# A two-layer hybrid transformer on one core: log sigmoid with tokens on partitions, queries split in place, keys' tiles exchanged, and the first sum of squares taken tile by tile

## The chip, the core and the metric

The kernel runs on one core of one Trainium2 chip. The metric is device time in microseconds; lower is better. The engines of a core work through queues of their own, in order: TensorE (matrix products, with a separate queue entry for loading weights), VectorE, ScalarE, GpSimd, and SyncE, which here only issues DMAs. In the profile they are PE (and PEld for weight loads), DVE, ACT, POOL and SP. Everything is float32 in and out.

## The reference, cut to what matters

There are 512 tokens of width 1024 and two layers. Every layer is a norm, a mixing part, a norm, and a gated feed-forward part with a short convolution.

```python
def rmsnorm(x, g):
    y = xf * lax.rsqrt(jnp.mean(xf * xf, axis=-1, keepdims=True) + EPS) * g

# layer 0: 8 heads of "fox" attention and 8 heads of sparse attention (dsa)
log_f = jax.nn.log_sigmoid(ff + b_fox_f)          # 512 tokens x 8 heads
c = jnp.cumsum(log_f, axis=1)                     # over tokens
s = einsum(q, k) * scale + c_q - c_k              # fox: decay between query and key
score = einsum(iw, relu(einsum(iq, ik)))          # dsa: an index over keys, per query
_, sel = lax.top_k(score, 128)                    # only the best 128 keys take part
# layer 1: 16 heads of block attention (moba); with 512 tokens it is causal softmax attention
mq, mk = apply_partial_rope(mq), apply_partial_rope(mk)
```

A partial rotation (rope) by position is applied to the queries and keys of the dsa and moba heads and of the index, but not to the fox heads.

## The kernel before, in words

Features lie on partitions and tokens along the free axis: x is `xT`, eight tiles of 128 features by 512 tokens. Since float32 products go through TensorE as two reduced-precision halves, every operand is split into a high part (a cast on ScalarE) and a low part (the remainder, a subtraction on VectorE or GpSimd), and a product is three matmuls: high by high, high by low, low by high (`mm3`, lines 159 to 161). `proj` makes 128 output features for all tokens with 24 such matmuls of 512 columns. Its result lies in one of three PSUM tiles with the tag `mm`.

The norm is not applied to x ahead of the products. `prep` (lines 171 to 177) scales x by the gain and splits it into `xh` and `xl`; the factor per token, one over the root of the mean square, is multiplied in when a product leaves PSUM (`scaled`, or in `rope` through the tables `CR` and `SR`, which are the cosine and sine tables times that factor). The factor is made by `rstd_of`: four transposes of the sum of squares, a sum over the free axis, a handful of small VectorE instructions for the root (lines 195 to 201), and four transposes that spread it over the partitions.

At the start (lines 563 to 590) the eight tiles of x arrive by DMA. `rope_angles` reduces position times frequency to an angle with some 26 small VectorE instructions on 128x32 and 128x64 and takes the sine; `rope_tables` writes these into tables and transposes them. `square` sums squares of tiles 0 to 3 on GpSimd, the loop behind it those of 4 to 7 on VectorE, and `rstd_main` makes the factor. The first projection (`misc`) holds the index key, the shared rope key, the forget gate in rows 96 to 103 and the index weights in rows 104 to 107. `ym` is this tile after rope.

The log sigmoid of the forget gate is computed on rows 96 to 127 of `ym`, 512 tokens along the free axis (lines 645 to 655): absolute value, exponential, logarithm with a correction, then a running sum over tokens. The result and its remainder are copied into four groups of 32 rows of the tile `ck`, which enters the fox scores as a matmul of its own (line 344).

Heads are worked in pairs, two heads of 64 rows in one projection. `stack_q` makes two tiles from a pair's queries, each with one head's high parts in one half of the partitions and its low parts in the other: a cast and a subtraction over 128 rows, and three DMAs that move halves across partitions. `stack_k` makes four tiles from the keys with six DMAs: head 0 uses the tile in which the parts were made, once its upper half is overwritten, and head 1 a tile filled by two DMAs. `scores` (lines 268 and 269) then needs two matmuls per block. The DMAs are issued on SP's queue, as are the loads of weights.

`heads` writes a software pipeline: scores and softmax of one head, then projections of the next pair, then the mix of the head before. The index scores and the selection of 128 keys (`select`, VectorE's max and replace instructions, lines 629 and 630) are put between the fox heads. The instructions are written in this order, but their order in each engine's queue is set by a planner: it goes through the program with a cost model and gives each engine, of the instructions it believes ready, the one written first. At run time the queues are strictly in order.

## Time and profile before

| | us |
|---|---|
| median of 3 runs | 1263.99 (1262.1 to 1265.39) |
| the profiled execution | 1261.51, of it 1259.7 from its first to its last instruction |
| TensorE busy | 1220.4 (97%) |
| VectorE busy | 810.9 (64%) |
| ScalarE busy | 557.4 (44%) |
| GpSimd busy | 357.7 (28%) |

The attention part of the first layer lasts until about 265 us of the span, its feed-forward part until about 640, the attention part of the second layer until about 870, and its feed-forward part to the end. Busy time is a union of instructions; idle time in front of an instruction stands in brackets behind it with what ended it.

### The profile page before, as it was taken

The numbers are of one execution on the slowest core, as the hardware profiler recorded it, in microseconds if no ns is written. First come the engines' busy times: TensorE is split into PE (matmuls) and PEld (weight loads), VectorE is DVE, ScalarE is ACT, GpSimd is POOL, SyncE is SP. The second block draws the span as 40 slices with busy tenths as digits, with TensorE's granted clock in tenths as the row PEclk, the third lists the DMA queues.
The fourth block names the chain that finished last, engine by engine and source line by source line (L and its number), as shares of the span: only waits on it lengthen the run. The fifth ranks groups of instructions, "written<-read, shape, count | busy, mean of one in ns | idle before, by whom it ended". The sixth has DMA issues, their size and how long they took to land.

```text
span 1259.7 us, 16807 instructions
## 1 busy us (share of the span) xinstructions
PE 1220.4 (97%) x5996; PEld 1018.3 (81%) x5996; DVE 810.9 (64%) x1489; ACT 557.4 (44%) x969; POOL 357.7 (28%) x394
## 2 busy tenths in 40 slices
PE   6889999999999999999999999999999999999997
PEld 4768778778888888888887888888888888888887
DVE  7889988675654555544666778787655555444555
ACT  5564667653332333333445556555433333332334
POOL 3665557542111111111213223332222111111110
PEclk9989999999999999999999999999999999999999
DMA  5333444222333322323325434331233332333321
GB/s 194 101 92 111 128 99 128 63 80 89 101 100 100 98 90 93 96 93 100 103 96 142 113 100 123 105 109 67 84 93 108 100 100 92 94 100 101 96 88 67
DMA packets 57379, 127.24 MB, mean 101 GB/s; under 512 B 7584, under 2 KB 21024, under 8 KB 57296
## 3 DMA queue, kind: packets, MB, share of 16 engines
q1 hardware_dynamic: 56368, 124.81, 33.2%
q10 hardware_dynamic: 864, 1.17, 0.3%
q8 instruction: 47, 0.77, 0.2%
q14 instruction: 36, 0.29, 0.1%
q0 software_dynamic: 64, 0.20, 0.0%
HBM read 104.13 MB, written 2.10 MB: 84 GB/s over the span
## 4 chain that ended last, share of the span: by engine, by line
PE 79%; DVE 10%; issue 5%; ACT 3%; DMA 2%; POOL 1%; POOLq 0%; ACTq 0%; DVEq 0%; SPq 0%
PE mm_g L160 6%; PE mm_g L161 6%; PE mm_g L159 6%; PE mm_u L161 6%; PE mm_u L159 6%; PE mm_u L160 6%; PE mm_d L161 6%; PE mm_d L160 6%; PE mm_d L159 6%; DVE tmask L630 2%; DVE m L629 1%; DMA mq_l<-mq_h 1%; PE t_m L372 1%; PE o_m L381 1%; PE mm_mk L160 1%
## 5 line engine op out<-in xcount | busy, mean ns | idle before, releaser
L434 POOL TENSOR_TENSOR cv<-cv,gs 128x512 f32<-128x512 f32 x44 | 57.1, 1298 | 546.2 <-ACT gs L433 546.2
L159 PE MATMUL mm_d<-a_h,wh_d 128*128 128x512 f32 (+1 forms) x384 | 142.8, 372 | 0.0
L160 PE MATMUL mm_d<-a_l,wh_d 128*128 128x512 f32 (+1 forms) x384 | 142.6, 371 | 0.0
L161 PE MATMUL mm_d<-a_h,wl_d 128*128 128x512 f32 (+1 forms) x384 | 142.6, 371 | 0.0
L503 DVE TENSOR_TENSOR us<-mm_u,cv 128x512 f32<-128x512 f32 x44 | 30.4, 692 | 168.1 <-PE mm_u L161 132.7
L160 PE MATMUL mm_g<-xl,wh_g 128*128 128x512 f32 x352 | 137.2, 390 | 0.4 <-DVE xl L175 0.4
L159 PE MATMUL mm_u<-xh,wh_u 128*128 128x512 f32 x352 | 137.3, 390 | 0.0
L161 PE MATMUL mm_u<-xh,wl_u 128*128 128x512 f32 x352 | 137.0, 389 | 0.0
L160 PE MATMUL mm_u<-xl,wh_u 128*128 128x512 f32 x352 | 137.0, 389 | 0.0
L161 PE MATMUL mm_g<-xh,wl_g 128*128 128x512 f32 x352 | 137.0, 389 | 0.0
L159 PE MATMUL mm_g<-xh,wh_g 128*128 128x512 f32 x352 | 137.0, 389 | 0.0
L148 ACT CAST wh_g<-raw_g 128x1024 fp32r<-128x1024 f32 x44 | 46.3, 1052 | 143.1 <-PE mm_g L160 141.6
L500 DVE TENSOR_TENSOR gs<-mm_g,RB 128x512 f32<-128x512 f32 x44 | 30.4, 691 | 118.2 <-PE mm_g L161 115.7
L128 ACT CAST wh_d<-raw_d 128x1024 fp32r<-128x1024 f32 x45 | 47.4, 1054 | 123.7 <-PE mm_u L160 103.4
L160 PEld LDWEIGHTS mm_d<-a_l,wh_d 128*128 128x128 f32 x384 | 72.3, 188 | 12.5
L159 PEld LDWEIGHTS mm_d<-a_h,wh_d 128*128 128x128 f32 x384 | 72.3, 188 | 12.5
L161 PEld LDWEIGHTS mm_d<-a_h,wl_d 128*128 128x128 f32 x384 | 72.3, 188 | 12.4
L160 PEld LDWEIGHTS mm_g<-xl,wh_g 128*128 128x128 f32 x352 | 66.1, 188 | 14.8 <-DVE xl L175 1.1
L161 PEld LDWEIGHTS mm_u<-xh,wl_u 128*128 128x128 f32 x352 | 66.1, 188 | 13.8
L159 PEld LDWEIGHTS mm_g<-xh,wh_g 128*128 128x128 f32 x352 | 66.1, 188 | 13.7
L161 PEld LDWEIGHTS mm_g<-xh,wl_g 128*128 128x128 f32 x352 | 66.1, 188 | 13.7
L160 PEld LDWEIGHTS mm_u<-xl,wh_u 128*128 128x128 f32 x352 | 66.1, 188 | 13.6
(778 smaller groups left out, 3072.4 us busy)
## 6 DMA issues: line engine op xcount, KB each, us to landing
raw_g<-in_w SPq DMA_DIRECT2D x44, 512.0 KB, 3.5
raw_u<-in_w SPq DMA_DIRECT2D x44, 512.0 KB, 3.6
raw_d<-in_w SPq DMA_DIRECT2D x41, 256.0 KB, 2.9
raw_d<-in_w SPq DMA_DIRECT2D x29, 192.0 KB, 2.6
raw_d<-in_w SPq DMA_DIRECT2D x34, 128.0 KB, 2.4
raw_oe<-in_w SPq DMA_DIRECT2D x8, 512.0 KB, 4.0
raw_mv<-in_w SPq DMA_DIRECT2D x8, 512.0 KB, 3.5
raw_mk<-in_w SPq DMA_DIRECT2D x8, 512.0 KB, 4.0
```

Source lines behind the costliest of these rows:

```text
L128: A.copy(dst_h, src)
L148: A.copy(wh, raw)
L159: PE.matmul(out, ah, bh, start=first, stop=False)
L160: PE.matmul(out, ah, bl, start=False, stop=False)
L161: PE.matmul(out, al, bh, start=False, stop=last)
L372: PE.transpose(t[:, n * P:n * P + P], probs[i][:, j * P:j * P + P], ident)
L381: PE.matmul(o[:, o0:o0 + w], vj, ph[:, c0:c0 + w], start=j == 0, stop=False)
L434: G.tensor_tensor(cv, cv, gs, op=OP.mult)
L500: V.tensor_tensor(gs, og, RB, op=OP.mult)
L503: V.tensor_tensor(us, ou, cv, op=OP.mult)
L629: V.max(m8, sc)
L630: V.match_replace(sc, m8, sc, -3e38)
```

## The change

At the start, a tile's square follows its scaling at once, the sums are all made on VectorE, and the square of the last tile is not added but enters as a second matmul against a column of ones, which also takes the place of the four transposes and of the sum over the free axis. `rope_angles` is written after the norm. The last tiles' second accumulator goes.

The gate's bias is added to rows 96 to 127 of `ym` in place, so that the gate comes out of the transposes that were there for the index weights, with tokens on partitions and 4 x 8 numbers in each. The log sigmoid is made in this form, written four times side by side into a tile, and brought back by four new transposes; the running sum reads PSUM.

`split_q` makes the two query tiles without DMAs: for each, a cast of one head's 64 rows and a subtraction that writes the other half of the partitions. The first fox pair and all eight moba pairs use it; the other fox pairs, the dsa pairs and the index queries keep `stack_q`. In `stack_k` the roles of the tiles are exchanged for all pairs: head 0 gets the tile filled by the first two DMAs, head 1 the one in which the parts were made.

```diff
             A.activation(s, xT[:, d], AF.Square)
             (V if d == KT - 1 else G).tensor_tensor(acc, acc, s, op=OP.add)
 
-    def rstd_of(acc, n, nm, nb=NB):
+    def rstd_of(acc, n, nm, nb=NB, more=None):
+
 
         st = ps("T", f"st_{nm}")[:, :nb * P]
-        for b in range(nb):
-            PE.transpose(st[:, b * P:b * P + P], acc[:, b * P:b * P + P], ident)
         ms, y, h, t = (col(f"{c}_{nm}", nb) for c in ("ms", "y", "h", "t"))
-        V.reduce_sum(ms, st.rearrange("p (b c) -> p b c", b=nb), axis=mybir.AxisListType.X)
+        if more is None:
+            for b in range(nb):
+                PE.transpose(st[:, b * P:b * P + P], acc[:, b * P:b * P + P], ident)
+            V.reduce_sum(ms, st.rearrange("p (b c) -> p b c", b=nb), axis=mybir.AxisListType.X)
+        else:
+            for b in range(nb):
+                s = slice(b * P, b * P + P)
+                PE.matmul(st[:, 2 * b:2 * b + 2], acc[:, s], ones, start=True, stop=False)
+                PE.matmul(st[:, 2 * b:2 * b + 2], more[:, s], ones, start=False, stop=True)
+            ms, st = ms.rearrange("p (b c) -> p b c", c=1), st[:, :2 * nb].rearrange("p (b c) -> p b c", c=2)
+            tc.keep_in_program_order(V.tensor_copy(ms, st[:, :, 0:1]))
+            ms = ms.rearrange("p b c -> p (b c)")
         V.tensor_scalar(ms, ms, 1.0 / n, EPS, op0=OP.mult, op1=OP.add)
         V.tensor_scalar(t.bitcast(I32), ms.bitcast(I32), 1, None, op0=OP.logical_shift_right)
         V.tensor_scalar(y.bitcast(I32), t.bitcast(I32), -1, 0x5F3759DF, op0=OP.mult, op1=OP.add)
...
 
     scale = {}
 
-    def rstd_main(acc, nm):
-        y, bc = rstd_of(acc, D, nm)
+    def rstd_main(acc, nm, more=None):
+        y, bc = rstd_of(acc, D, nm, more=more)
         A.copy(RB, bc)
         r = cp.tile([P, NB], F32, name=f"rstd_{nm}")
         V.tensor_copy(r, y)
...
         move(l[LO], h[HI])
         return a, l
 
+    def split_q(y, nm):
+
+        q = big(f"{nm}_a"), big(f"{nm}_b")
+        for t, s, o in ((q[0], LO, HI), (q[1], HI, LO)):
+            A.copy(t[s], y[s])
+            V.tensor_tensor(t[o], y[s], t[s].bitcast(F32), op=OP.subtract)
+        return q
+
     def stack_k(y, nm, eng=V):
+
 
         out = []
         for n, t in zip("hl", halves(y, nm, eng)):
             b = big(f"{nm}_b{n}")
-            move(b[LO], t[HI])
-            move(b[HI], t[HI])
-            move(t[HI], t[LO])
-            out += [t, b]
+            move(b[LO], t[LO])
+            move(b[HI], t[LO])
+            move(t[LO], t[HI])
+            out += [b, t]
         return out[0], out[1], out[2], out[3]
 
     def scores(out, q, k, e, qs, w, first=True):
...
         nc.sync.dma_start(xT[:, d], xT_d[:, d])
     nc.gpsimd.dma_start(const, const_d)
     G.tensor_copy(cmask[:, 384:], const[:, C_TRI:C_TRI + P])
-    cs = rope_angles()
+    sq = None
     for d in range(KT):
         prep(d, 0, None)
+        sq = acc if d == 0 else tmp(f"sq{d}")
+        A.activation(sq, xT[:, d], AF.Square)
+        if 0 < d < KT - 1:
+            V.tensor_tensor(acc, acc, sq, op=OP.add)
     pmisc = proj("misc", w)
     w = [chunk("iq0")]
-    acc2 = tmp("acc2")
-    for d in range(KT):
-        if d < 4:
-            square(d, acc)
-        else:
-            s = acc2 if d == 4 else tmp(f"sq{d}")
-            A.activation(s, xT[:, d], AF.Square)
-            if d > 4:
-                V.tensor_tensor(acc2, acc2, s, op=OP.add)
-    V.tensor_tensor(acc, acc, acc2, op=OP.add)
+    rstd_main(acc, "n0", sq)
+    cs = rope_angles()
     w.append(chunk("iq1"))
     V.tensor_copy(selr[0:96, :P], const[0:96, C_SEL:C_SEL + P])
     V.tensor_copy(selr[96:128, :P], const[64:96, C_SEL:C_SEL + P])
     V.tensor_scalar(selr[:, P:], const[:, C_FSEL:C_FSEL + 8], 0.5, None, op0=OP.mult)
     rope_tables(cs)
-    rstd_main(acc, "n0")
     rope_scaled()
 
     ym = rope(pmisc, "misc")
...
     G.memset(kr[0:64].bitcast(F32), 0.0)
     split(kr[64:96], kr[96:128], ym[64:96])
     iwT = cp.tile([P, NB, 4], F32, name="iwT")
+    R = slice(96, 128)
+    A.activation(ym[R], ym[R], AF.Identity, bias=vec[R, V_BF:V_BF + 1])
     t = ps("T", "iwps")
     for b in range(NB):
         PE.transpose(t[:, b * P:b * P + P], ym[:, b * P:b * P + P], ident)
-    A.activation(iwT, t.rearrange("p (b c) -> p b c", b=NB)[:, :, 104:108], AF.Copy, scale=0.0625)
+    t = t.rearrange("p (b c) -> p b c", b=NB)
+    A.activation(iwT, t[:, :, 104:108], AF.Copy, scale=0.0625)
+
+    fg = tmp("fg")
+    la, lm, lu = (fg[:, k * 32:k * 32 + 32].rearrange("p (b h) -> p b h", b=NB) for k in range(3))
+    A.activation(la, t[:, :, 96:104], AF.Abs)
+    V.tensor_scalar(lm, t[:, :, 96:104], 0.0, None, op0=OP.min)
     iq = [stack_q(rope(proj(f"iq{h}", w[h]), f"iq{h}"), f"iq{h}") for h in range(2)]
 
 
...
     ckv = halves(yn, "ckv")
 
 
-    R = slice(96, 128)
-    la, lm, lu = tmp("la"), tmp("lm"), tmp("lu")
-    bf = vec[R, V_BF:V_BF + 1]
-    A.activation(la[R], ym[R], AF.Abs, bias=bf)
-    V.tensor_scalar(lm[R], ym[R], bf, 0.0, op0=OP.add, op1=OP.min)
-    A.activation(la[R], la[R], AF.Exp, scale=-1.0)
-    V.tensor_scalar(lu[R], la[R], 1.0, None, op0=OP.add)
-    V.scalar_tensor_tensor(la[R], lu[R], -1.0, la[R], op0=OP.add, op1=OP.subtract)
-    A.activation(lu[R], lu[R], AF.Ln)
-    V.tensor_tensor(lm[R], lm[R], lu[R], op=OP.subtract)
-    V.tensor_tensor(lm[R], lm[R], la[R], op=OP.add)
-    V.memset(la[R], 1.0)
-    V.tensor_tensor_scan(lu[R], la[R], lm[R], 0.0, op0=OP.mult, op1=OP.add)
+    A.activation(la, la, AF.Exp, scale=-1.0)
+    V.tensor_scalar(lu, la, 1.0, None, op0=OP.add)
+    V.scalar_tensor_tensor(la, lu, -1.0, la, op0=OP.add, op1=OP.subtract)
+    A.activation(lu, lu, AF.Ln)
+    V.tensor_tensor(lm, lm, lu, op=OP.subtract)
+    le, one = tmp("le"), tmp("one")
+    G.memset(le, 0.0)
+    G.memset(one, 1.0)
+    for b in range(NB):
+        e = le[:, b * P:b * P + P].rearrange("p (g c) -> p g c", g=4)[:, :, 0:8]
+        V.tensor_tensor(e, lm[:, b:b + 1].to_broadcast([P, 4, 8]), la[:, b:b + 1].to_broadcast([P, 4, 8]), op=OP.add)
+    t = ps("T", "ckps")
+    for b in range(NB):
+        PE.transpose(t[:, b * P:b * P + P], le[:, b * P:b * P + P], ident)
+    lc = tmp("lc")
+    V.tensor_tensor_scan(lc, one, t, 0.0, op0=OP.mult, op1=OP.add)
     ck = big("ck")
-    A.copy(ck[R], lu[R])
-    ckt = tmp("ckt")
-    V.tensor_tensor(ckt[R], lu[R], ck[R].bitcast(F32), op=OP.subtract)
-    for r in (0, 64):
-        A.copy(ck[r:r + 32], lu[R])
-        V.tensor_copy(ck[r + 32:r + 64], ckt[R])
+    A.copy(ck, lc)
+    for r in (32, 96):
+        V.tensor_tensor(ck[r:r + 32], lc[r:r + 32], ck[r:r + 32].bitcast(F32), op=OP.subtract)
 
     lo_on_pool = True
     fo, do, ukv = [], [], []
...
             values["f", p // 2] = v_group(f"fv{p // 2}_")
 
         def qs():
-            c["q"] = stack_q(scaled(proj(f"fq{p}"), f"fq{p}"), f"fq{p}")
+            c["q"] = (stack_q if p else split_q)(scaled(proj(f"fq{p}"), f"fq{p}"), f"fq{p}")
 
         def ks():
             c["k"] = stack_k(scaled(proj(f"fk{p}"), f"fk{p}"), f"fk{p}", G)
...
             values["m", p // 2] = v_group(f"mv{p // 2}_", moba_scale if p == 0 else None)
 
         def qs():
-            c["q"] = stack_q(rope(proj(f"mq{p}"), f"mq{p}"), f"mq{p}")
+            c["q"] = split_q(rope(proj(f"mq{p}"), f"mq{p}"), f"mq{p}")
 
         def ks():
             c["k"] = stack_k(rope(proj(f"mk{p}"), f"mk{p}"), f"mk{p}")
```

## Rows read from the trace of the kernel before

**Rows 1.** Busy us by stretch: PE, PEld, DVE, ACT, POOL, PEclk, DMA share, GB/s.

```profile
0.00:40.00 40.00, 27.15 (x101) 20.48 (x102) 31.05 (x82) 21.28 (x33) 14.59 (x25) 0.96 0.49 165
...
67.00:90.00 23.00, 19.71 (x78) 15.20 (x77) 18.47 (x59) 15.39 (x29) 16.98 (x18) 0.87 0.35 98
90.00:170.00 80.00, 76.25 (x437) 64.68 (x437) 74.94 (x199) 43.15 (x101) 47.66 (x69) 0.99 0.39 108
...
640.00:680.00 40.00, 36.90 (x211) 31.25 (x210) 28.28 (x64) 16.34 (x32) 7.19 (x8) 1.00 0.46 129
680.00:860.00 180.00, 177.11 (x1031) 152.56 (x1030) 137.32 (x308) 103.13 (x238) 54.49 (x72) 1.00 0.39 107
```

**Rows 2.** Waits of TensorE, whole span: us in total, times, longest us.

```profile
PE mm_misc L159 <- ACT wh_misc L128: 6.6, 1, 6.6
PE mm_misc L160 <- DVE xl L175: 3.5, 1, 3.5
PE s_f L268 <- DMA fq_a<-fq_l: 3.3, 1, 3.3
PE s_m L268 <- DMA mq_l<-mq_h: 3.3, 3, 1.3
PE bc_n L204 <- DVE y_n L201: 3.1, 4, 2.2
PE ix L268 <- ACT rl L618: 2.3, 1, 2.3
...
PE s_m L268 <- DMA mq_a<-mq_l: 1.0, 1, 1.0
```

**Rows 3.** Timeline of TensorE: start us, us, instruction, [idle before <-releaser].

```profile
37.51 0.40 PE L159 MATMUL mm_ckv<-xh,wh_ckv 128*128 128x512 f32 x1
...
84.57 0.58 PE L268 MATMUL s_f<-fk_h,fq_a 128*128 128x256 f32 x1 [3.29 <-DMA fq_a<-fq_l]
...
88.26 0.63 PE L269 MATMUL s_f<-fk_l,fq_a 128*128 128x512 f32 x1
88.68 0.63 PE L161 MATMUL mm_fk<-xh,wl_fk 128*128 128x512 f32 x1
...
91.24 0.39 PE L159 MATMUL mm_fq<-xh,wh_fq 128*128 128x512 f32 x1
91.47 0.39 PE L160 MATMUL mm_fq<-xl,wh_fq 128*128 128x512 f32 x1
```

**Rows 4.** Timeline of the other engines, 0 to 45 us.

```profile
4.83 0.72 ACT L174 ACTIVATE xh<-xT,vec 128x512 fp32r<-128x512 f32 x1 [1.69 <-DMA vec<-in_vec]
...
5.77 0.19 DVE L293 TENSOR_TENSOR ang_x<-vec,posf 128x32 f32<-128x32 f32 x1
...
12.46 1.31 POOL L186 TENSOR_TENSOR acc<-acc,sq 128x512 f32<-128x512 f32 x1 [0.57 <-ACT sq L185]
...
12.57 1.76 DVE L175 SCALAR_TENSOR_TENSOR xl<-xT,vec,xh 128x512 fp32r<-128x512 f32 x1
...
17.77 0.75 DVE L175 SCALAR_TENSOR_TENSOR xl<-xT,vec,xh 128x512 fp32r<-128x512 f32 x1
...
34.00 0.69 DVE L217 TENSOR_TENSOR CR<-CT,RB 128x512 f32<-128x512 f32 x1 [1.48 <-ACT RB L211]
```

**Rows 5.** Timeline of VectorE, 45 to 67 us, four rows of the log sigmoid.

```profile
52.11 0.48 DVE L647 TENSOR_SCALAR lm<-ry_misc,vec 32x512 f32<-32x512 f32 x1
...
59.29 1.61 DVE L655 TENSOR_TENSOR_SCAN lu<-la,lm 32x512 f32<-32x512 f32 x1
...
61.59 1.08 DVE L659 TENSOR_TENSOR ckt<-lu,ck 32x512 f32<-32x512 f32 x1 [0.17 <-ACT ck L657]
62.70 1.27 DVE L662 CAST ck<-ckt 32x512 fp32r<-32x512 f32 x2
```

**Rows 6.** Timeline, 74 to 86 us: the first fox pair's queries.

```profile
76.74 1.17 DVE L129 TENSOR_TENSOR fq_l<-sc_fq,fq_h 128x512 fp32r<-128x512 f32 x1
...
80.14 0.59 SPq L244 DMA_DIRECT2D fq_a<-fq_l  x1
```

**Rows 7.** The tile mq_l: duration ns min/median/max, first and last start us.

```profile
L129 DVE TENSOR_TENSOR mq_l<-ry_mq,mq_h x8: 654/691/694, 665.4 to 829.7; 128x512 fp32r<-128x512 f32 x8
```

## The prediction

> **What bounds the kernel now.** I read the busy time by stage first. TensorE is busy in 27.15 of the first 40 us, in 19.71 of the 23 us from 67 to 90, in 36.90 of 40 from 640 to 680 and in 177.11 of 180 from 680 to 860, and its mean granted clock is 0.96 and 0.87 of full speed in the first two [rows 1]. From 90 to 170 VectorE is as full as TensorE: 74.94 of 80 against 76.25 [rows 1]. So TensorE sets the end, and a change that leaves its work alone wins time only where it stands still or runs slowly, which is mostly in the first 90 us; and one stretch has a second engine that is nearly as full.
>
> The list of TensorE's waits comes next [rows 2]. It names 3.5 us for the low parts of x at the start, 3.3 us for the first head pair's queries by DMA, 3.3 + 1.0 us for queries of the odd layer by DMA, up to 2.2 us in one piece for the root of a norm, and 2.3 us for a relu on ScalarE in the index scores. Each of these is in a place that the change touches.
>
> Last the clock, in TensorE's own timeline: after the wait that ends at 84.57 a 512-column matmul takes 0.63 us and starts 0.42 us after the one before, further on 0.39 and 0.23 [rows 3]. The mean granted clock of a stretch prices this: one minus it, times the length, is what the lower of the two levels (1.2 instead of 2.4 GHz) cost: 0.04 x 40 = 1.6 us at the start, 0.13 x 23 = 3.0 us from 67 to 90 [rows 1].
>
> **The change part by part.**
>
> *Squares summed as the tiles come, the angles behind the norm.* Today GpSimd adds the first squares, and beside such an addition VectorE's low part of x takes 1.76 us where it takes 0.75 alone [rows 4]. TensorE waits 3.5 us for just these parts [rows 2]. The GpSimd additions go. VectorE gets six additions of 128x512 where it had four (+2 x 0.69 us, the length of the CR row [rows 4]), and the 26 or so small angle instructions (0.19 us for 128x32 [rows 4]) sink below them. ScalarE paces the tiles: one scaled copy and one square each, at most 0.72 [rows 4] apiece, so eight pairs last 11.5 us; the first starts at 4.83, and the last low part is done at 4.8 + 10.8 + 0.75 = 16.4 to 17.1, instead of 18.5 (17.77 + 0.75 [rows 4]). Twenty-four matmuls of the first projection at the slow spacing of 0.42 [rows 3], from 6.6 on, last until 16.7. So the projection ends some 2 to 3 us earlier.
>
> The norm then starts at 17 to 18. Its twelve small VectorE instructions at 0.19 us give the row factor by about 21. But CR and SR now wait for the angles too. If none of these found a hole among the tiles they follow the norm: 26 instructions and eight table writes at 0.19 are 6.5 us, sine, transposes and copies I price at five ScalarE instructions of 0.72 (no row shown here has the table load), so CR starts at about 31; if most find a hole, at 25. Today it starts at 34.0 [rows 4]. CR frees the PSUM tile for the fourth projection, which starts at 37.51 now [rows 3]. TensorE's own bound for that start is 17 + 48 x 0.23 + about 2 us of transposes = 30. So the gain lies between 2.5 us (angles last, and some of the wait back) and 7.5. I take 4: nearest to the 2.2 us wait [rows 2] and its 1.6 us of clock, which surely lie behind the norm.
>
> *Log sigmoid with tokens on partitions.* Ten VectorE instructions on 32x512, from 52.11 to 63.97, take 8.4 us; the scan is 1.61 and the remainder of ck 1.08 of it [rows 5]. After the change there are four on 128x32 at 0.19 [rows 4], four broadcasts of the same price, one scan and two remainders: 0.8 + 0.8 + 1.6 + 2.2 = 5.4 us. The scan now reads PSUM; no row shows that, and I bound it by 1.61 as it is and by 0.69 (a row of 128x512 [rows 4]) more. ScalarE loses two of three copies of ck; in that queue the relu stood behind them, so the 2.3 us wait of the index scores [rows 2] goes. In return TensorE gets four transposes in the middle of its queue that wait for a VectorE chain, and behind them stand projections of the fox layer that cannot overtake. Such a wait is not in the trace; the nearest is 2.2 us for the norm's root [rows 2]. Bounds 0 and 2.2; I take 1, half way, since this chain is short. The bias added in place puts one ScalarE instruction (0.72 at most) ahead of the transposes of the index weights; with it the bound is 2.9. Net -1.3.
>
> *Queries split in place, first fox pair.* Now the remainder ends at 77.9, its DMA is issued at 80.14, behind other work on SP's queue [rows 6], and lands in time for 84.57 [rows 3]. After: two half-height casts and two half-height subtractions. No row here has half height; I price it as full, 0.72 and 1.17 [rows 4, 6], so the pair ends at 77.9 + 1.9 = 79.8, before TensorE runs out of other work at 81.3 (84.57 less 3.29). The 3.3 us [rows 2] go, and with them the 3.0 us of clock [rows 1]: 6.3. Next late are the readers of the scores on VectorE, busy 18.47 of 23 us here [rows 1]. I take 5, with 3.3 and 6.3 as the ends.
>
> *Queries of the odd layer, eight pairs.* The waits of 3.3 and 1.0 [rows 2] go with their DMAs. Price: eight more subtractions (0.69 [rows 7]) and casts (0.72), 5.5 us of VectorE in 180 us of which it idles 42.7 [rows 1]. Next late are the keys, whose DMAs go out before the queries'. 4.3 us in all; I take 4, with 0 and 4.3 as the ends.
>
> At this place a rule of the Trainium skill speaks against the change: SBUF — State Buffer, Who interferes with whom, says that a VectorE instruction with two SBUF inputs and a GpSimd instruction that reads SBUF exclude each other, the later one waiting for the end of the first. The low part at 1.76 beside 0.75 agrees [rows 4]; the eight subtractions at 654 to 694 ns do not show it here [rows 7]. What it would do is rival (c).
>
> *First heads' keys in own tiles.* The same six DMAs per pair in another order: head 0 waits for two that start at once, head 1 for the one behind. No wait of [rows 2] is for a key, so 0; what the second head waits longer, the softmax of the first covers, and without that cover it is one DMA, as the queries' was.
>
> *TensorE's own work.* Four transposes for ck, and eight two-column matmuls for four transposes: eight narrow ones more, each between 0 and the 0.23 of a 512-column one [rows 3]. I take +0.9.
>
> *What is given back.* TensorE comes to 90 some 10 us earlier, into 80 us in which VectorE has 5 us free [rows 1]. VectorE comes earlier too, by its own start (2.5 or more), by 3.0 us of log sigmoid and by the shorter wait for scores, and pays 0.7 to 1.2 for the second subtraction. Nearly in step; I give back 1.5, between 0 and the 4 that rival (a) has.
>
> Sum: -4 - 1.3 - 5 - 4 + 0.9 + 1.5 = -11.9 us. The profiled execution took 1261.51 (its span is 1259.7), which makes 1249.6; the median of the runs, 1263.99, lies 2.5 above it, and from there the same sum gives 1252.1. I forecast 1251.
>
> **Rivals.**
> (a) VectorE holds the front: from 90 to 170 the top-k selection keeps it busy, and TensorE's earlier arrival turns into new waits. Of the front's 10.3 - 0.9 only VectorE's own gain in log sigmoid, 3.0, and some of its start stay: -3 to -5, with the odd layer -7 to -9 less part of it: 1255 to 1259. For: 74.94 of 80. Against: log sigmoid leaves this same queue.
> (b) It does not do what it says: the order of instructions is planned anew, and queries that no longer wait for a DMA stand behind other work of VectorE, so that TensorE's waits change names and keep their length: 1261 to 1266. For: VectorE is long in demand in each of these places. Against: a DMA of 2 to 4 us is gone in any order.
> (c) Slower: in the odd layer VectorE's subtractions wait for GpSimd, ahead of the softmax's reductions in the same queue. Each of a pair's two, blocked as the low part of x was (1.76 - 0.75 = 1.0 [rows 4]), costs 1.7, and the second cast 0.72: about 4 us a pair that TensorE's scores and the next head's reductions stand behind. It decides from 2 us a pair on: eight pairs then lose 16 against the 10 of the front, and lose 32 at the full price, of which VectorE's idle 42.7 [rows 1] hides half or more: 1268 to 1273. This is what the rule of the Trainium skill above would bring. Against: 0.69 in all eight rows [rows 7].
>
> **How the numbers follow.** Forecast 0.66; (a) 0.17; (b) 0.10; (c) 0.07. With each term at its end the forecast reaches from -7.5 - 2.3 - 6.3 - 4.3 + 0.9 = -19.5, 1242 on the profiled time, to -2.5 + 0.6 - 3.3 + 1.8 = -3.4. What a measurement can tell from no change is about 0.3%, 3.8 us. Faster: the forecast and (a), 0.83; same: (b), 0.10; slower: (c), 0.07. The range of eight in ten holds the forecast, (a) and the near end of (b): 1241 to 1262.
>
> **What would show it.** Right: no wait for the DMAs of fq and mq, and a clock of 1 from 67 to 90; the first projection done by 18 us, the fourth started by 33; no relu wait near 61; query subtractions at 0.7. Wrong: a TensorE wait for CR's end, or one over 2.2 us for the new transposes of ck; new waits between 90 and 170 that add up to what the first 90 us won; query subtractions over 1.2 us; an odd layer whose scores still stand behind queries or, in their place, keys.

## The result, and the profile after

The changed kernel is slower. Its median is 1270.71 us (1270.5 to 1273.77, 6 runs) against 1261.51 for the kernel before (6 runs on the same chip): a ratio of 1.0071 with a 95% interval of 1.0055 to 1.0086. The forecast was 1251, in a range of 1241 to 1262. The profiled execution took 1270.85, its span 1269.1.

TensorE's waits in the changed kernel (us in total, times, longest us), to set against [rows 2]:

```profile
PE mm_misc L159 <- ACT wh_misc L128: 6.4, 1, 6.4
PE s_f L287 <- DMA fq_a<-fq_l: 3.7, 3, 1.7
PE mm_dq L159 <- DVE dv L129: 3.2, 2, 2.0
...
PE o_d L400 <- ACT pt_d_0h L128: 2.8, 2, 2.4
PE s_m L287 <- DVE mq_a L270: 2.7, 4, 1.2
PE tabT L345 <- DVE exp_tab L342: 2.3, 1, 2.3
PE bc_kv L214 <- DVE y_kv L211: 1.7, 1, 1.7
...
PE mm_fv__1_494 L159 <- DVE ry_iq L236: 1.4, 1, 1.4
...
PE ix L287 <- ACT rl L640: 1.0, 2, 0.7
...
PE mm_misc L160 <- DVE xl L175: 0.6, 2, 0.3
```

Each wait that the change aimed at is gone or smaller: xl 3.5 to 0.6, the relu 2.3 to 1.0, the first pair's DMA 3.3 to nothing, the odd layer's DMAs 4.3 to nothing. Others stand in their place, and one bears the old name: fq_a now holds TensorE up three times, in later pairs.

The same stretches as in [rows 1], with two more in the dense part of the first layer (PE, PEld, DVE, ACT, POOL busy, PEclk, DMA share, GB/s):

```profile
0.00:40.00 40.00, 30.10 (x124) 22.78 (x125) 27.11 (x86) 23.66 (x37) 10.88 (x24) 0.96 0.52 172
67.00:90.00 23.00, 21.18 (x97) 16.53 (x96) 22.08 (x74) 18.41 (x38) 21.78 (x25) 1.00 0.39 102
90.00:170.00 80.00, 72.76 (x407) 61.37 (x405) 68.89 (x174) 37.41 (x86) 40.26 (x57) 0.96 0.39 104
...
190.00:215.00 25.00, 20.61 (x107) 16.61 (x106) 16.17 (x39) 13.61 (x34) 16.32 (x21) 0.93 0.44 115
...
680.00:860.00 180.00, 174.91 (x1017) 149.88 (x1017) 144.09 (x308) 104.36 (x238) 66.77 (x73) 1.00 0.34 96
```

From 67 to 90 the clock is whole, as forecast (0.87 before). From 90 to 170 TensorE does less than before (72.76 against 76.25) at a lower clock, and so does VectorE (68.89 against 74.94): both stand still more often. So VectorE, less full than before, is not what newly holds that stretch.

Where the time came from is plainest at landmarks of TensorE's timeline (start us in the profiled execution, or end where said; the last two columns are kernels from below):

| | before | changed | after_held | after_heldall_rope_ls |
|---|---|---|---|---|
| fourth projection (mm_ckv) | 37.51 | 35.21 | 35.20 | 33.41 |
| index scores (ix) | 57.40 | 58.47 | 58.42 | 56.24 |
| first fox output (o_f) | 99.86 | 95.51 | 94.06 | 91.88 |
| first dense scores (s_d) | 177.05 | 176.92 | 170.31 | 166.71 |
| last dense query projection, end | 212.76 | 220.26 | 213.44 | 206.83 |
| first feed-forward part (mm_g) | 275.98 | 283.59 | 276.76 | 270.31 |
| odd layer's last output (o_m), end | 867.37 | 876.47 | 869.88 | 863.36 |

The changed kernel is 2.3 us ahead at the fourth projection and 1.1 behind at the index scores. By the first fox output it is 4.4 ahead, and by 177 all of that is handed back. From there to 220 another 7.6 are lost; the odd layer loses 1.5.

Each column is one execution, and a landmark moves from one execution to the next: before, only_q0, only_mq and only_k, in which the start is unchanged, have the fourth projection at 35.66 to 37.55.

One place shows how. These are the second fox pair's queries. First SP's queue (start us, us to issue), then what was issued from 91 to 103 us with the time to landing, then the matmul that waits:

```profile
96.05 0.33 SPq L147 DMA_DIRECT2D raw_fq<-in_w  x1
96.43 0.46 SPq L254 DMA_DIRECT2D fq_a<-fq_h  x1
96.95 0.59 SPq L254 DMA_DIRECT2D fq_a<-fq_l  x1
```

```profile
raw_fq<-in_w SPq DMA_DIRECT2D x1, 512.0 KB, 4.3
...
fq_a<-fq_h SPq DMA_DIRECT2D x1, 128.0 KB, 4.4
fq_a<-fq_l SPq DMA_DIRECT2D x1, 128.0 KB, 4.2
fq_l<-fq_h SPq DMA_DIRECT2D x1, 128.0 KB, 2.2
```

```profile
101.23 0.38 PE L287 MATMUL s_f<-fk_bh,fq_a 128*128 128x256 f32 x1 [1.68 <-DMA fq_a<-fq_l]
```

The low part was done at 94.72, but its transfer went out only at 96.95: ahead of it on SP's queue stands a load of 512 KB for a later head, which itself waits until GpSimd's subtraction has freed its buffer (at 96.03). And then the transfer takes 4.2 us, where the third one, issued when the load has landed, takes 2.2. In the kernel before, the pair at this place had its transfers ahead of that load (issued at 99.35 and 100.41, 2.2 us each) and waited for nothing. There it was the first pair whose transfers stood behind a load, [rows 6]. So the change took the transfers out of that pair, and the new order put the next pairs' behind a load instead. The Trainium skill gives a reason (DMA: Bandwidth & Descriptors, Queues, rings and completion order): the DMAs that SP issues share one row of rings, and each DMA engine takes their descriptors in ring order. The trace agrees: 4.2 to 4.4 us right behind the load, 2.2 without one. It shows the times, not the rings.

This is theory Q: the change reorders SP's queue, and queries' transfers behind weight loads make the loss. Its rival S: the new order costs elsewhere (VectorE, norms, values), and the fq_a waits only take up slack.

### The profile page after: what moved, and what is told of

It reads as the page before. It is cut to its first block, busy times and chain, and to the rows that moved or that the text cites. A ratio compares the mean times of both kernels' runs of the same rounds, so it can differ in the third digit from the quotient of the medians.

```text
span 1269.1 us, 16797 instructions
## 1 busy us (share of the span) xinstructions
PE 1224.6 (96%) x6012; PEld 1018.5 (80%) x6012; DVE 813.7 (64%) x1501; ACT 560.1 (44%) x977; POOL 365.2 (29%) x393
```

## The experiments

All runs in one table. The ratio is to the kernel before, run beside it on the same chip. The last column counts, in each profile, how many of the fq_a and dq_a transfers (two for each pair stacked by DMA) were issued within 1.3 us behind a weight load. A profile is of one execution; those of before_held, before_rope and after_heldall took 2.7 to 3.3 us longer than the medians.

| kernel | median us | ratio, 95% | behind a load |
|---|---|---|---|
| before | 1261.4 to 1262.1 | | 5 of 16 |
| changed | 1270.71 | 1.0071 [1.0055, 1.0086] | 9 of 14 |
| only_start | 1272.49 | 1.0077 [1.0048, 1.0106] | 9 of 16 |
| only_log | 1268.12 | 1.0044 [1.0027, 1.0060] | 5 of 16 |
| only_q0 | 1265.97 | 1.0034 [1.0017, 1.0051] | 6 of 14 |
| only_mq | 1263.90 | 1.0005 [0.9991, 1.0020] | 5 of 16 |
| only_k | 1260.24 | 0.9994 [0.9982, 1.0007] | 5 of 16 |
| after_held | 1264.46 | 1.0026 [1.0010, 1.0041] | 4 of 14 |
| before_held | 1267.20 | 1.0047 [1.0031, 1.0064] | 4 of 16 |
| start_held | 1263.87 | 1.0019 [1.0008, 1.0029] | 3 of 16 |
| log_held | 1267.79 | 1.0049 [1.0034, 1.0063] | 6 of 16 |
| after_held_rope | 1267.42 | 1.0049 [1.0036, 1.0062] | 7 of 14 |
| nomq_held_rope | 1265.48 | 1.0029 [1.0016, 1.0042] | 7 of 14 |
| before_rope | 1270.01 | 1.0076 [1.0060, 1.0091] | 8 of 16 |
| after_heldall | 1267.86 | 1.0042 [1.0026, 1.0057] | 0 of 14 |
| after_heldall_rope | 1260.66 | 0.9986 [0.9977, 0.9996] | 0 of 14 |
| nomq_heldall | 1269.62 | 1.0056 [1.0040, 1.0071] | 0 of 14 |
| before_heldall | 1261.72 | 0.9996 [0.9982, 1.0009] | 0 of 16 |
| after_heldall_rope_ls | 1259.06 | 0.9973 [0.9961, 0.9985] | 0 of 14 |
| before_heldall_rope | 1259.26 | 0.9975 [0.9962, 0.9988] | 0 of 16 |

The last column does not put the times in order. only_log has the 5 of the kernel before and is 6 us slower; of the kernels with 0, the fastest takes 1259 and the slowest 1270 us. Nor are their transfers all free: in each of these six, one or two transfers of the first or second fox pair were issued 2.3 to 3.3 us behind a load and took 3.3 to 4.6 us.

**One part at a time.** Each is the kernel before with one part of the diff above.

only_start, the squares, the norm and the angles:

```diff
+    rstd_main(acc, "n0", sq)
+    cs = rope_angles()
```

> The kernel before with the new start alone (squares tile by tile, angles behind the norm). Theory Q (the loss is the order of SP's queue: in the plan of this kernel a weight load stands ahead of the query DMAs of the second fox pair): 2 us won up to 50 us, then a TensorE wait of 1 to 2 us for fq_a near 100 and some 2 us of low clock behind it; 1260 to 1264 where before has 1261.5. Theory S (the new start is harmless, the loss is elsewhere): no such wait, 1257 to 1259.

1272.49, slower than either theory had it and no faster than the whole change. TensorE waits for fq_a in three pairs (2.5, 1.3 and 2.1 us), 4.7 us for dv, 2.6 for the key norm's squares.

only_log, the new log sigmoid:

```diff
+    t = ps("T", "ckps")
+    V.tensor_tensor_scan(lc, one, t, 0.0, op0=OP.mult, op1=OP.add)
```

> The kernel before with the new log sigmoid alone. In its plan the query DMAs of the second fox pair stand ahead of the weight load, as before. Theory Q: no wait for fq_a near 100, the relu wait of 2.3 us gone, 1258 to 1261. Theory L (the loss comes from the longer path to the key norm, whose waits grew from 1.9 to 3.4 us between 40 and 55): these waits are here too, 1262 to 1266.

1268.12, above both theories. Two pairs wait for fq_a (2.6 and 2.5), and 2.5 us are lost before the key norm's factor.

only_q0, the first fox pair's split:

```diff
+            c["q"] = (stack_q if p else split_q)(scaled(proj(f"fq{p}"), f"fq{p}"), f"fq{p}")
```

> The kernel before with the queries of the first fox pair split in place, nothing else. In its plan the weight load stands ahead of the query DMAs of the second fox pair. Theory Q: the wait at 84.57 goes (6 us with its clock) and comes back as a wait for fq_a of the second pair, 1260 to 1265. Rival (the split itself is good, other parts lose): 1255 to 1257.

1265.97, 1 us above Q's range. The wait at 84.57 is gone, and two others (2.2 at 103.4, 2.7 at 161.1) have come: 4.9 us where 3.3 were taken away. This part alone is the clearest case of a wait that moved.

only_mq, the odd layer's split:

```diff
+            c["q"] = split_q(rope(proj(f"mq{p}"), f"mq{p}"), f"mq{p}")
```

> The kernel before with the queries of the odd layer split in place, nothing else; the order of the first layer is that of before. Theory V (the added subtractions meet GpSimd's softmax scaling: in the changed kernel GpSimd is busy 12 us longer here): waits for mq_a by VectorE and for the transposes take the place of the DMA waits, 1262 to 1264. Rival (the 4.3 us of DMA waits are won here, and the loss of 1.5 us in this layer comes from the keys' order): 1257 to 1259.

1263.90, in theory V's range and no change that can be told, where the prediction had 4 us of gain for it.

only_k, the keys' tiles:

```diff
+            move(b[LO], t[LO])
+            move(t[LO], t[HI])
+            out += [b, t]
```

> The kernel before with the keys of the first heads in tiles of their own, alone. The prediction had 0 for it, and it leaves the order of the first layer's instructions as it was: 1261 to 1263 and no landmark of the odd layer moved by over 1 us. If the keys' new order of transfers is a part of the odd layer's loss, 1263 to 1265.

1260.24: nothing, as predicted. So three parts, each alone, make the kernel slower, and the other two do nothing.

**Weight loads behind the fox pairs' transfers.** The instructions stay the same, and four loads are issued later on SP. The rest is planned anew around them: in after_held some 60 of TensorE's instructions changed places too, in log_held over 170 (counted as the fewest that have to move).

```diff
+    HOLD = {"fq2": "fq0", "fq3": "fq1", "dq2": "fq2", "oe0_0": "fq3"}
-        nc.sync.dma_start(raw, w_d[idx[name]])
+            with tc.issue_after(behind):   # behind the second transfer of that pair
+                nc.sync.dma_start(raw, w_d[idx[name]])
```

> The changed kernel with one thing more: the loads of the weights for the heads that come later (512 KB each: those of the fox queries 2 and 3, of the third dense queries and of the first output tile) are issued on SP's queue only behind the two transfers that stack the queries of the fox pair being worked on. Same arithmetic, same transfers. Theory Q (the loss in the first layer is a place in SP's queue: the query transfers of the fox pairs 1 to 3 stand behind a 512-KB load there and beside it land in 4.3 instead of 2.2 us): the waits of 1.68, 1.70 and 0.27 us for fq_a go, and with the first two some 2 us each of low clock behind them; 7 to 8 us, so 1262 to 1265, and no TensorE wait for fq_a over 0.3. Theory S (the order planned anew costs the time in other places: VectorE between 90 and 215, the dense queries, the values, and the fq_a waits only take up slack): 1268 to 1272.

1264.46: 6 of the 9 us come back, as theory Q said, and the fourth pair's wait and the third's are gone. The transfers of the third pair, issued from 127 to 133 us:

```profile
fq_a<-fq_h SPq DMA_DIRECT2D x1, 128.0 KB, 2.2
fq_a<-fq_l SPq DMA_DIRECT2D x1, 128.0 KB, 2.2
fq_l<-fq_h SPq DMA_DIRECT2D x1, 128.0 KB, 3.5
```

One wait of 1.5 us is left, against Q's 0.3: the second pair's transfers, issued at 93.82 and 94.73, run beside a load of 91.54 and take 4.8 and 4.2 us.

> The new start alone (squares summed as the tiles come, angles behind the norm), with the same weight loads behind the query transfers. Theory Q: the waits for fq_a of 2.47, 1.34 and 2.14 us in the new start alone go with their low clock: from 1272.5 by 10 to 12 us, so 1260 to 1263. Theory S: the start's own new order (a wait for the tables, for the norm of the keys, 4.7 us for the dense values' VectorE) keeps it: 1267 to 1273.

1263.87 from 1272.49, within 1 us of Q, and no wait for fq_a is left.

> The kernel before, with the same weight loads behind the query transfers as in after_held, and nothing else. Theory Q: pair 0's wait of 3.29 us for fq_a at 84.57, which stood behind such a load too (transfers issued at 80.14, 2.2 us after the low part was done, landed 4.4 us later), shrinks to under 1, and the low clock behind it goes: 3 + 2.5 us, so 1256 to 1259. Theory S: what arrives earlier at 85 is handed back up to 215, or the later loads make new waits for weights: 1261 to 1266.

1267.20, a miss: the wait at 84.57 shrinks to 0.4, as Q said, but the dense queries now wait 4.3 us for their own transfers (dq_a).

> The new log sigmoid alone, with the same weight loads behind the query transfers. Theory Q: the waits for fq_a of 2.60 and 2.48 us go with some 3 us of low clock: from 1268 to 1259 to 1262, no slower than the kernel before. Theory S: 1266 to 1269, since the wait of 2.5 us for a norm's factor at 53.8 and what stands behind it is the loss.

1267.79, a miss of Q and in S's range: the pairs no longer wait, the 2.6 us before the key norm stay, waits for probabilities grow from 3.3 to 5.4, and 2.9 for dq_a are new, in the most reordered of the four. So Q holds place by place, and rival S is right that a freed place is not yet a gain.

**Rope products ahead of weights on GpSimd.** after_held had won 6.7 us by the first dense scores and gave them back by 213. GpSimd's subtraction for later weights stands ahead of a query's rope product there, VectorE waits for the product, and TensorE for what is queued on VectorE. The same is seen at 40 us in the changed kernel, GpSimd first, then VectorE:

```profile
36.90 2.83 POOL L152 TENSOR_TENSOR wl_fv<-raw_fv,wh_fv 128x256 fp32r<-128x256 f32 x4 [3.46 <-ACT wh_fv L148]
39.69 2.53 POOL L237 TENSOR_TENSOR rs_iq<-rs_iq,SR 128x512 f32<-128x512 f32 x2
```

```profile
41.02 1.75 DVE L238 TENSOR_TENSOR ry_iq<-ry_iq,rs_iq 128x512 f32<-128x512 f32 x1 [2.32 <-POOL rs_iq L237]
```

The edit, again of order alone; against after_held only four rows move in GpSimd's order and three in SP's, and none on the other three engines (a row is one instruction, or up to four subtractions for one weight). In before_rope some 20 of TensorE's instructions move too. The expectations further down that name six, or eight and four, rows count each row where it left and where it came.

```diff
+    ROPED = {"fv0_1": "iq1", "dq2": "dq0", "dq3": "dq1", "oe0_0": "dq2", "oe0_2": "dq3"}
+                    with tc.issue_after(first):   # behind the rope product of that query
                         G.tensor_tensor(wl[:, t], raw[:, t], wh[:, t].bitcast(F32), op=OP.subtract)
```

> The changed kernel with the weight loads held as in after_held, and one thing more on GpSimd's queue: the weight parts of fv0_1, dq2, dq3, oe0_0 and oe0_2 are split only behind the rope products of iq1, dq0, dq1, dq2 and dq3. Same instructions. after_held had won 6.7 us over the kernel before by the first dense scores (170.31 against 177.05) and lost 7.4 of them again by the last dense query. Theory R (GpSimd's queue: the rope product of a query stands behind the split of weights that wait for ScalarE and TensorE, VectorE waits for the product, and behind it stand the evictions and probabilities that TensorE waits for): the waits mm_dq<-dv (3.5), o_d (2.9) and mm_fv<-ry_iq (1.5) shrink to under half, and the low clock behind 200 us goes: 4 to 8 us, so 1257 to 1261. Theory T (from 170 to 215 the stretch has a floor of its own, VectorE or the weights' arrival, and earlier work is handed back in any order): 1262.5 to 1266.

1267.42, worse: theory R fails as it was put. The waits for dv (3.5 to 2.1) and ry_iq shrink, but TensorE now waits here:

```profile
PE s_d L302 <- DMA dq_a<-dq_h: 3.9, 3, 2.3
PE bc_kv L229 <- DVE y_kv L226: 3.6, 1, 3.6
...
PE s_d L302 <- DMA dq_a<-dq_l: 2.2, 1, 2.2
```

And what was issued from 186.5 to 196 us shows Q's pattern once more, in the dense queries:

```profile
raw_oe<-in_w SPq DMA_DIRECT2D x1, 512.0 KB, 4.7
...
dq_a<-dq_h SPq DMA_DIRECT2D x1, 128.0 KB, 4.8
dq_a<-dq_l SPq DMA_DIRECT2D x1, 128.0 KB, 4.7
dq_l<-dq_h SPq DMA_DIRECT2D x1, 128.0 KB, 2.2
```

> The kernel before, with the rope products of iq1 and dq0 to dq3 ahead of the weight parts as in after_held_rope, and with nothing held on SP's queue. There TensorE waited for dv once (1.8 us at 168.6) and for nothing else that stands behind a rope product. Theory R: that wait and its 1.6 us of low clock go, 1 to 3.5 us: 1258.5 to 1261. Theory T: 1261 to 1263.

1270.01, a miss by 9 us: a few GpSimd instructions in another order, and what the planner moved with them, cost the kernel before as much as the whole change did. Its profile has 5.0 us of waits for dq_a, which the kernel before does not have, and 3.4 for fq_a (3.3 there).

> As after_held_rope, but the odd layer's queries are stacked by DMA as in the kernel before. If the split of the odd layer's queries costs what its own trace said (+1.7 us in the odd layer of only_mq, +1.5 in the changed kernel), this is 1.0 to 2.5 us below after_held_rope. By the prediction's own reckoning, which gave the split a gain of 4, it would be 4 above. With theory R it is 1255 to 1259.5 and so faster than the kernel before; with theory T 1261 to 1264.5.

1265.48, 1.9 below after_held_rope, as expected of the odd layer's split (but see nomq_heldall).

**All queries' transfers ahead.** The four loads for the output tiles are held behind the dense pairs' transfers as well:

```diff
-    HOLD = {"fq2": "fq0", "fq3": "fq1", "dq2": "fq2", "oe0_0": "fq3"}
+    HOLD = {"fq2": "fq0", "fq3": "fq1", "dq2": "fq2", "oe0_0": "dq0",
+            "oe0_1": "dq1", "oe0_2": "dq2", "oe1_0": "dq3"}
```

> The changed kernel with the weight loads held behind the query transfers of the fox pairs as in after_held, and those of the output tiles oe0_0, oe0_1, oe0_2 and oe1_0 behind the query transfers of the four dense pairs too. Theory Q (a query's transfers lose 2 us wherever a 512-KB load is issued right ahead of them): the wait of 1.1 us for dq_a goes, and no transfer of dq_a takes over 3 us; the rest of the dense stretch (mm_dq<-dv 3.5, o_d 2.9) stays: 1261.5 to 1264. Theory L (the loads that go out later make the weights of the output projection late): a wait for wh_oe or wl_oe of over 1 us appears: 1264 to 1267.

1267.86, over both theories. The dq_a wait is gone and each of these transfers takes 2.2 us, as Q said; no wait for weights came, against L. What grew is o_d (2.9 to 4.9); with the rope products ahead, in the next kernel, it is 2.0.

> As after_heldall, with the rope products ahead of the weight parts on GpSimd, as in after_held_rope (1267.4, whose dense scores waited 6.1 us for dq_a). Theory Q: these 6.1 us and some 1.7 us of low clock from 190 to 215 go: 1258.5 to 1261.5, and it is the rope order with the transfers free that keeps the 7 us. Theory T (the stretch from 170 to 215 has a floor of its own): the waits take another name, 1263 to 1267.

1260.66, as Q said: 10 us below the changed kernel, by order alone. Each of the two edits alone made after_held 3 us worse, and both together make it 4 better; from after_heldall to here, 7.2 us hang on seven moved rows of GpSimd and SP. The dense stretch with both:

```profile
170.00:190.00 20.00, 19.55 (x108) 15.59 (x107) 16.23 (x42) 15.72 (x41) 12.61 (x18) 1.00 0.27 59
190.00:215.00 25.00, 24.68 (x136) 19.60 (x134) 20.06 (x52) 17.71 (x44) 15.82 (x22) 1.00 0.54 146
```

From 190 to 215 TensorE is busy in 24.68 us, in the changed kernel in 20.61, at a whole clock instead of 0.93. (The dense scores start at 170.75 here and at 176.92 there, so the two windows do not hold quite the same work.)

> The kernel before with all these loads held, fox and dense. before_held was at 1267.2, with 4.3 us of waits for dq_a. Theory Q: these and the 3.2 us for fq_a of the kernel before are both gone: 1257 to 1261. Theory L: 1263 to 1268, waits for wh_oe or dv instead.

1261.72, level with the kernel before; Q's gain of 1 to 4 is not there, though its profile has no wait for dq_a and 0.3 us at most for fq_a.

> As after_heldall, with the odd layer's queries stacked by DMA as in the kernel before: 1.5 to 2.5 us below after_heldall if the odd layer's loss is the split; with theory Q 1259 to 1262, with theory L 1262 to 1265.

1269.62, 1.8 above after_heldall where 2 below was expected. So the split's cost, read from two pairs of kernels, has both signs.

**The last two.** The new log sigmoid's three small VectorE instructions go behind the key norm:

```diff
+    with tc.issue_after(last["kv"]):   # the last instruction of the key norm's root
         V.tensor_scalar(lu, la, 1.0, None, op0=OP.add)
         V.scalar_tensor_tensor(la, lu, -1.0, la, op0=OP.add, op1=OP.subtract)
```

> As after_heldall_rope, with the three VectorE instructions of the log sigmoid that come before its sum issued behind the root of the key norm: six rows of VectorE's order change, none of another engine. Theory N (the norm stands behind the log sigmoid): the wait bc_kv <- y_kv falls from 3.5 to 2 or less and the index scores start 1 to 2 us earlier than at 60.8, and with the low clock from 40 to 67 (0.94) the kernel is at 1257 to 1260. Theory G (the norm's small instructions are slow beside GpSimd's subtraction of the weights, 1.57 instead of 0.17 us for 128x4, and the subtraction would only come at another moment): bc_kv stays over 2.8 and the time at 1260 to 1262.

1259.06 and theory N for the most part: the wait bc_kv falls from 3.5 to 2.2, the index scores start at 56.24 instead of 60.78 (1.7 us of which this profile had already at the fourth projection), and the clock from 40 to 67 is whole, where after_heldall_rope had 0.94:

```profile
40.00:67.00 27.00, 23.73 (x160) 21.06 (x159) 23.88 (x55) 13.46 (x25) 18.16 (x24) 1.00 0.41 112
```

> The kernel before with the weight loads held (as in before_heldall, 1261.7) and the rope products ahead of the weight parts; eight rows of GpSimd's order and four of SP's change against before_heldall, none of TensorE, VectorE or ScalarE. If the two orders are worth as much to the kernel before as to the changed one (7.2 us between after_heldall and after_heldall_rope), 1254 to 1257, and the change is a loss of 4 to 6 us even in order. If the kernel before has nothing to gain there (before_rope was 8.6 slower, all of it in transfers that are now free), 1260 to 1263, and the change is worth nothing in either direction.

1259.26. The kernel before gains 2 us from the same orders, neither 5 to 7 nor nothing. Both kernels in order are 0.27% and 0.25% faster than the kernel before, intervals 0.9961 to 0.9985 and 0.9962 to 0.9988, and level with each other: the change itself is worth nothing that these runs can tell. The comparison is not quite even, though. The changed kernel has one edit more here, and without it (after_heldall_rope, 0.9986) it is 0.11% above; and the orders were chosen from the changed kernel's waits.

## Why the prediction was wrong, step by step

The step that failed is the reckoning of what is given back: 1.5 us, and only by VectorE between 90 and 170; and, in rival (b), the sentence that "a DMA of 2 to 4 us is gone in any order". The transfers of one pair were gone, but the order of SP's queue is planned anew with every edit, and the next pairs' transfers came to stand behind loads. By the landmarks, 4.2 us are given back from 96 to 177, and 7.6 more are lost from 177 to 220, a stretch for which the sum has no term.

That order makes this loss is shown: with the same instructions, other orders bring the changed kernel from 1270.71 to 1260.66 and 1259.06, 10 and 12 us, as much as the whole gain forecast. How much of it is transfers behind loads is not settled. after_held gives back 6 of the 9 us, but after_heldall, with fewer transfers behind loads, only 2.9. Rival (b) named the mechanism, but its range ended at 1266, since it let waits change their names and not grow. The forecast's weak end, -3.4, is said to have each term at its end, but leaves what is given back at 0, though its own bound was 4.

- **Start, -4.** The low parts of x end at 17.03 (16.4 to 17.1 predicted), CR starts at 30.33 (25 to 31), the fourth projection at 35.21: -2.3, just under the small end of 2.5 to 7.5. Over all profiles it starts at 34.7 on the mean in the ten with the new start, and at 37.4 in the ten without: -2.7. The wait of 2.3 us for exp_tab is the "angles last" of that end. What failed is that it would last: by the index scores at 58.47 it is a loss of 1.1. The way from one landmark to the other is 1.1 and 1.8 us longer than before in the two kernels with the new start alone (only_start, start_held), and the log sigmoid makes it longer still (next).
- **Log sigmoid, -1.3.** The instructions are as cheap as forecast, and the term is wrong in sign for the way to the index scores. On VectorE the four additions, the scan and the two remainders below take 4.0 us, and four small ones 0.9 more, against 8.4 for ten instructions before [rows 5] and 5.4 forecast; the scan out of PSUM is 1.22, less than either bound:

```profile
52.49 0.49 DVE L675 TENSOR_TENSOR le<-fg 128x32 f32<-128x32 f32 x4
53.55 1.22 DVE L680 TENSOR_TENSOR_SCAN lc<-one,ckps 128x512 f32<-128x512 f32 x1 [0.57 <-PE ckps L678]
...
55.70 2.29 DVE L684 TENSOR_TENSOR ck<-lc,ck 32x512 fp32r<-32x512 f32 x2
```

  The relu's wait fell from 2.3 to 1.0, and the new transposes brought none. What was not priced are the small instructions, which the planner moved ahead of the key norm. In the changed kernel one of them waits on VectorE for ScalarE's logarithm, and the norm's sum stands behind it:

```profile
47.59 0.34 DVE L669 TENSOR_TENSOR fg<-fg 128x32 f32<-128x32 f32 x1 [1.00 <-ACT fg L668]
47.85 0.68 DVE L196 TENSOR_REDUCE ms_kv<-st_kv 128x4 f32<-128x512 f32 x1
```

  From the fourth projection to the index scores, TensorE has the same work in all kernels but for the four new transposes of ck, and in the kernels with the new start alone the four of the index weights, which come earlier. The ten profiles with the new log sigmoid take 22.8 to 25.7 us there, the ten without it 19.9 to 21.7; alone (only_log) it makes 23.9 of 19.9. The bound set for new waits was 2.9. With the small instructions behind the norm (after_heldall_rope_ls) it is 22.8. By the first fox output only_log is no more than 0.3 us late.
- **First fox pair, -5.** Nearly right where it stands. With this part alone (only_q0) the wait at 84.57 is gone, the clock from 67 to 90 is whole, and the first fox output comes 2.5 us earlier with 13 more value matmuls of 256 columns done by then, at 0.12 us each: 4.0 us. Handed back as told.
- **Odd layer, -4.** Wrong in sign. The 4.3 us of DMA waits became 2.7 us for mq_a on VectorE, and those for probabilities grew from 0.8 to 2.5. From the last matmul of the gate projection (mm_g) in the first feed-forward part to the first in the second, the seven profiles with the split take 282.97 to 283.17 us, and the thirteen without it 280.15 to 285.03, with a mean of 282.0 (before: 281.44). So the split makes this layer steadier and, on the mean, 1 us longer; single profiles can't tell that from chance, nor do the medians.
- **Keys, 0.** Right.
- **Rival (a), VectorE holds the front.** No: VectorE is less busy from 90 to 170 than before.
- **Rival (c), GpSimd blocks the subtractions.** Both engines are slower where rival (c) said, and its price was far too high. The half-height subtractions take 791 and 867 ns on the mean, where a full-height one took 691 [rows 7]; GpSimd's scaling of probabilities, groups by line (busy us, mean ns), goes from 685 to 926 ns for 128x128:

```profile
L353 POOL TENSOR_SCALAR prt_m<-prt_m,sm_m 128x128 f32<-128x128 f32 x16 | 11.0, 685 | 75.6 <-DVE sm_m L351 69.1 <-PE mm_oo__4_7980 L161 5.0 <-PE s_m L268 1.4
```

```profile
L372 POOL TENSOR_SCALAR prt_m<-prt_m,sm_m 128x128 f32<-128x128 f32 x16 | 14.8, 926 | 72.1 <-DVE sm_m L370 72.1
```

  In all seven profiles with the split this scaling takes 829 to 926 ns, in the thirteen without it 663 to 692. That fits the rule of the Trainium skill that the prediction cited (SBUF — State Buffer, Who interferes with whom), at 0.1 to 0.25 us an instruction on the mean and not at the 1.0 that was reckoned.

What stays open: in after_heldall_rope_ls, 10.3 us are won by the first dense scores and 5.9 by the last dense query projection. The stretch between the two takes 35.4 to 35.7 us in the kernel before, only_mq and only_k, whose first layers have the same order, and 37.8 to 46.1 in all the others. So every other order tried has lost 2 us or more here; which waits make it, and whether some orders only leave more of the work for this stretch, was not taken apart.

## What to carry to other kernels

Where the order of the queues is planned for the whole kernel, an edit's price is not its own instructions: moving five groups of GpSimd's instructions, with what the planner moved along, cost the kernel before 8.6 us, as much as the five parts of the change. Nor does an order have a price of its own: the same few rows of GpSimd and SP, with the order of the other engines unchanged, made after_held 3 us slower and after_heldall 7 us faster. Before a local gain is counted, look at what each queue will hold behind it, SP's above all: a small transfer that TensorE waits for must not be issued behind a large load that nobody waits for yet. When an edit turns out slower, put the old order back by hand before judging the edit.

## What was not expected of the hardware

Over the 20 profiles, 138 transfers of fq_a and dq_a were issued with no weight load under way, and took 2.16 to 2.31 us, with a median of 2.18. 83 were issued within 1.3 us behind a load of 512 KB and took 2.93 to 5.88, with a median of 4.42: 2.2 us more. The other 81 had a load under way that was issued longer before; their median is 2.42, and some take as long as those right behind a load. At the place shown above the load landed at 100.4 and the two transfers right behind it, at 100.8 and 101.2.

VectorE's smallest instructions can be slowed as well. In after_held_rope the key norm's second and third steps, 128x4, take 0.76 and 1.57 us, and the next ones 0.17. GpSimd subtracts weights from 44.61 on and then fills two tiles:

```profile
46.04 0.76 DVE L220 TENSOR_SCALAR ms_kv<-ms_kv 128x4 f32<-128x4 f32 x1
46.83 1.57 DVE L221 TENSOR_SCALAR t_kv<-ms_kv 128x4 int32<-128x4 int32 x1
48.43 0.17 DVE L222 TENSOR_SCALAR y_kv<-t_kv 128x4 int32<-128x4 int32 x1
```

```profile
44.61 2.84 POOL L164 TENSOR_TENSOR wl_fk<-raw_fk,wh_fk 128x256 fp32r<-128x256 f32 x4
47.37 0.54 POOL L686 MEMSET le<- 128x512 f32 x1
47.83 0.54 POOL L687 MEMSET one<- 128x512 f32 x1
```

The second of them ends at 48.40, when GpSimd has come to rest (48.37); from there each step takes 0.17. nomq_held_rope and after_heldall_rope show the same, with 1.58 us each. In the changed kernel, where the same steps run from 48.56 on, after that subtraction and beside the last memset, they take 0.28 and 0.17.
